# Dealing the first independent products of two pipelined stages out early instead of evenly

## The chip, the core and the metric

The kernel runs on one core of one Trainium2 chip. The metric is the device time of one execution in microseconds (us). Before the change the median of three runs is 1032.14 us (1031.85 to 1036.27). One more execution was profiled; that one took 1035.34 us, and its trace spans 1033.6 us.

## The reference, cut to what matters

One layer of a streaming encoder on 512 tokens of width 1024, all in float32:

```
x += 1/2 * SwiGLU_1(RMSNorm(x))
h  = RMSNorm(x); p = h @ W_in          # z, xbc, dt, q, k, v
     SSD: causal depthwise conv + SiLU on x/B/C, chunked scan over 16 heads, SiLU(z) gate, RMSNorm
     attention: 8 heads, own chunk + 8 previous chunks, clipped relative bias, softmax
x += concat(ssd_out, attn_out) @ W_out
x += 1/2 * SwiGLU_2(RMSNorm(x)); final RMSNorm
```

The change touches the middle only: the SSD scan and the attention, and the projections that are worked in beside them.

## The kernel before

Every float32 product is made of three matmuls on values split in a high and a low part: high by high, high by low, low by high (function `mm3`, lines 142, 143 and 144). Weights are split as they come: a cast on ScalarE writes the high part (`whi`, line 84), a subtraction on VectorE the low part (`wlo`, line 86). The weight stream `ws` splits three units ahead of their use and loads some units earlier still, by the SP queue (line 79).

The mixing stage has two halves. Each has a chain of steps whose matmuls wait for VectorE (DVE) and ScalarE (ACT), and each has a list of products that depend on no step of that chain. A generator yields after every six matmuls of such a product (or at its end, with its eviction); below, six matmuls are called a unit. An object `fill` of the class `Filler` is called at fixed places between the steps, and it takes units from the generator as they come due.

*SSD half.* There are eight steps: two head groups `g` by four chunks `c` of 128 tokens. Step by step the functions are `ssd_decay` (GpSimd, line 903, writes the tiles `fu` and `fh`), `ssd_in` (four transposes, line 914; eviction line 916; scaling of Y on ACT, line 922), `ssd_mask` (matmuls line 932, exponential line 934, DVE lines 937 to 944; from the second chunk on also line 954), `ssd_out` (lines 967 and 972; DVE 969, 977, 979) and `ssd_state` (line 987). The independent work (`fill1`) is B and C of the second group and the x columns 4 to 7 (each with a convolution: eviction line 839, ACT 845, three DVE operations of line 848, SiLU line 850), then v (`do_v`), z (gates, lines 886 to 889) and the first q and k columns. There are 87 units; 72 of them are dealt out over 35 calls, and a loop takes the other 15 at the end.

*Attention half.* There are 32 steps: eight heads by four query tiles of 128 rows, the longest first (i = 3, 2, 1, 0). `att_scores` makes the scores (lines 1189 and 1190), adds the bias and finds the row minimum (DVE, line 1193), takes the exponential (ACT, line 1197) and scales the rows (DVE, lines 1199 and 1200). Two steps later `att_transpose` transposes the result (line 1208), and ACT (line 1213) and DVE (line 1215) write its two parts; one more step later, at a head's end, `att_values` multiplies by v (line 1230; ACT 1232, DVE 1233, ACT 1234, DVE 1235). The bias of a head comes in the head's first step: a DMA issued by ACT (line 1176), then GpSimd (lines 1178 and 1179). The independent work (`fill2`) is four q and k products (16 units; evictions `do_qk`, lines 1023 to 1042), among whose last units the SSD output is scaled and split (lines 149 and 150), and the output projection of the SSD rows (32 units; evictions lines 1254 and 1255). These 48 units are dealt out over 64 calls. Before its first unit `fill2` starts the row norm of the SSD output (line 186), and it spreads it (line 205) after the fourth.

PSUM has three buffers `mm` for the products and five buffers `aux` for the chain. A tool orders each engine's instructions; TensorE (PE) stays close to the written order, while on DVE and ACT work of neighbouring steps is interleaved. Each engine works off its own instructions strictly in order.

Of the kernel before, what the change touches and what calls it, by code (L numbers as in the profile page):

```python
# [28 lines left out]
RATE1, RATE2, NPRE = 72, 48, 8  # L29
# [8 lines left out]
def hybrid_block(ctx: ExitStack, tc, xT, xt, par, wgu1, wd1, ws1, win, wdt, wv, wo, rbt, wgu2, ws2, fin, out):  # L38
# [6 lines left out]
    def sb(tag, shape, dt=F32, bufs=1):  # L45
        uid[0] += 1
        return pool.tile(shape, dt, tag=tag, name=f"{tag}_{uid[0]}", bufs=bufs)
# [41 lines left out]
    class Job:  # L89
# [3 lines left out]
        def __init__(self, split, *moves):  # L93
            self.split, self.moves, self.parts, self.holds = split, list(moves), None, self
# [52 lines left out]
    def split_act(src, wcol, hi, lo):  # L147

        S.activation(out=hi, in_=src, func=AF.Copy, scale=wcol)
        V.scalar_tensor_tensor(out=lo, in0=src, scalar=wcol, in1=f(hi), op0=ALU.mult, op1=ALU.subtract)  # L150
# [31 lines left out]
    def rstd_begin(acc, n):  # L182

        ps = aux()
        for t in range(NC):
            T.matmul(ps[:, t:t + 1], lhsT=acc[:, t * P:(t + 1) * P], rhs=ones[:, 0:1], start=True, stop=True)
        r = rstd_rows(ps, NC, n)
        return diag_parts(r, NC, sb("s51", [P, NC, P], F32R), sb("acc", [P, NC, P], F32R)), r
# [18 lines left out]
    def rstd_end(dg):  # L207

        pb = aux()
        spread(pb, dg)  # L210
        rs = sb("rstd", [P, SEQ], bufs=2)
        S.copy(out=rs, in_=pb)
        return rs
# [33 lines left out]
    def xw_slot(k):  # L247
        return lambda: xw_pair(k)
# [575 lines left out]
    def proj_gen(ah, al, done):  # L824

        ps = mmps()
        for k in range(KD):
            if k % 4 == 0:
                wh, wl = ws.get()
            mm3(ps, wh[:, k % 4], wl[:, k % 4], ah[k], al[k], k == 0, k == KD - 1)  # L830
            if k % 2 == 1 and k < KD - 1:
                yield
        done(ps)
        yield


    def conv(ci, dst, ps):
        u = sb("fa", [P, SEQ], bufs=3)
        V.tensor_tensor(out=u, in0=ps, in1=rs, op=ALU.mult)
        y = sb("fs", [P, SEQ], bufs=2)  # L840

        def cw(j):
            return pt[:, C_CW + 12 * j + ci:C_CW + 12 * j + ci + 1]

        S.activation(out=y, in_=u, func=AF.Identity, scale=cw(3), bias=pt[:, C_CB + ci:C_CB + ci + 1])
        for j in (2, 1, 0):
            d = 3 - j
            V.scalar_tensor_tensor(out=y[:, d:SEQ], in0=u[:, 0:SEQ - d], scalar=cw(j), in1=y[:, d:SEQ],
                                   op0=ALU.mult, op1=ALU.add)
        S.activation(out=dst, in_=y, func=AF.Silu)  # L850
# [3 lines left out]
    def bc(g):  # L854

        tiles = [slot(8 + 4 * g + i, None, F32) for i in range(2)]
        gens = [proj_gen(xh, xl, lambda ps, i=i: conv(8 + 2 * i + g, tiles[i], ps)) for i in range(2)]
        for i in (0, 0, 0, 1, 1, 1, 0, 1):
            next(gens[i], None)
            yield  # L860
        bf.append(tiles[0])
        cf.append(tiles[1])

    def bc_products(g):

        pa = aux()
        for c in range(NC - 1):
            T.transpose(out=pa[:, c * P:(c + 1) * P], in_=bf[g][:, c * P:(c + 1) * P], identity=ident)
        th = slot(10 + 4 * g, [P, NC - 1, P], F32)
        S.copy(out=th.rearrange("p c n -> p (c n)"), in_=pa[:, 0:384])  # L870
        btk.append(th)

        pa = aux()
        for c in range(NC):
            cs = slice(c * P, (c + 1) * P)
            T.matmul(pa[:, cs], lhsT=bf[g][:, cs], rhs=cf[g][:, cs], start=True, stop=True)
        t = slot(11 + 4 * g, [P, NC, P], F32)
        V.tensor_tensor(out=t, in0=pa.rearrange("p (c l) -> p c l", c=NC),
                        in1=tri.unsqueeze(1).broadcast_to([P, NC, P]), op=ALU.mult)
        cbm.append(t)  # L880
# [168 lines left out]
    def fill_by(names):  # L1049
        for t in names:  # L1050
            if t == 'v':
                yield from do_v()
            elif t[0] == 'z':
                yield from proj_gen(xh, xl, lambda ps: gate(int(t[1]), ps))
            else:
                yield from qk_gen(int(t[1]))

    def fill1():
        yield from bc(1)
        for i in range(4, 8):  # L1060
            yield from proj_gen(xh, xl, lambda ps: conv(i, Y[i], ps))
        yield from fill_by(FILL1)

    class Filler:
        def __init__(self, gen, total, slots):
            self.gen, self.rate, self.due = gen, total / slots, 0.0

        def __call__(self):
            self.due += self.rate
# [71 lines left out]
    T.matmul(pa[:, 0:64], lhsT=onesr, rhs=dal.rearrange("p c h -> p (c h)"), start=False, stop=True)  # L1141
    S.activation(out=cd.rearrange("p c h -> p (c h)"), in_=pa[:, 0:64], func=AF.Exp)
    steps = [dict(g=g, c=c) for g in range(2) for c in range(NC)]
    fill = Filler(fill1(), RATE1, 4 * 8 + 3)
    bc_products(0)
    ssd_decay(steps[0])
    fill()
# [89 lines left out]
    def fill2():  # L1237
        dg, _ = rstd_begin(acc3, D)
        gh, gl = [], []
        total = 8 * len(FILL2)  # L1240
        for n, _ in enumerate(fill_by(FILL2)):
            if n == total - 1 - KD // 2 - NPRE:
                rs3 = rstd_end(dg)

            for i in range(max(0, 2 * (n - total + KD // 2)), 2 * (n - total + KD // 2 + 1)):
                hi, lo = xw_slot(i)()
                split_act(Y[i], pt[:, C_SSD + i:C_SSD + i + 1], hi, lo)
                gh.append(hi)
                gl.append(lo)
            yield  # L1250

        def done(o, ps):
            t = sb("fa", [P, SEQ], bufs=3)
            V.tensor_tensor(out=t, in0=ps, in1=rs3, op=ALU.mult)
            V.tensor_tensor(out=x[:, o], in0=x[:, o], in1=t, op=ALU.add)

        for o in range(KD):
            yield from proj_gen(gh, gl, lambda ps: done(o, ps))

    steps = [dict(hd=hd, i=i) for hd in range(AH) for i in (3, 2, 1, 0)]  # L1260
    fill = Filler(fill2(), RATE2, 2 * len(steps))
    LAG, VLAG = 2, 1
    for n in range(len(steps) + LAG + VLAG):
        if n < len(steps):
# [166 lines left out]
```

## Time and profile before

| | us |
|---|---|
| median of three runs | 1032.14 |
| profiled execution | 1035.34 |
| its span | 1033.6 |
| TensorE (PE) busy | 1007.9 |
| VectorE (DVE) busy | 810.2 |
| ScalarE (ACT) busy | 587.8 |
| SSD half, with the loop at its end | about 391 to 555 |
| attention half | about 555 to 656 |

The profiled execution is 3.2 us longer than the median run. Times inside it are counted from the start of its span. A row of the timeline shows a start, a duration, the engine, the line, and in brackets how long the engine was idle before it and what ended that.

### The profile page before, as it was taken

The numbers are of one execution on the slowest core, as the hardware profiler recorded it, in microseconds if no ns is written. First come the engines' busy times: TensorE is split into PE (matmuls) and PEld (weight loads), VectorE is DVE, ScalarE is ACT, GpSimd is POOL, SyncE is SP. The second block draws the span as 40 slices with busy tenths as digits, with TensorE's granted clock in tenths as the row PEclk, the third lists the DMA queues.
The fourth block names the chain that finished last, engine by engine and source line by source line (L and its number), as shares of the span: only waits on it lengthen the run. The fifth ranks groups of instructions, "written<-read, shape, count | busy, mean of one in ns | idle before, by whom it ended". The sixth has DMA issues, their size and how long they took to land. (4 is left out here: it accounts for less than half of the span.)

```text
span 1033.6 us, 16129 instructions
## 1 busy us (share of the span) xinstructions
PE 1007.9 (98%) x6154; PEld 888.6 (86%) x6154; DVE 810.2 (78%) x1353; ACT 587.8 (57%) x926; POOL 163.7 (16%) x186
## 2 busy tenths in 40 slices
PE   8999999999999999999999999999999999999895
PEld 7889989998898777778878778879999899988884
DVE  7868876887676698978867999797688668876587
ACT  7555535654474456646656876666655356544445
POOL 1111121111110013323201111101211111111110
PEclk9999999999999999999999999999999999999988
DMA  8969989998652321222232223755898889988842
GB/s 309 290 160 210 218 185 228 224 203 211 147 122 91 102 82 62 71 73 69 71 98 71 82 83 102 230 131 128 191 211 209 196 209 231 209 213 202 167 107 99
DMA packets 48221, 162.66 MB, mean 157 GB/s; under 512 B 5264, under 2 KB 6032, under 8 KB 48144
## 3 DMA queue, kind: packets, MB, share of 16 engines
q0 software_dynamic: 16848, 60.04, 33.2%
q1 hardware_dynamic: 28992, 96.74, 27.1%
q10 hardware_dynamic: 2304, 4.86, 1.5%
q8 instruction: 48, 0.79, 0.3%
q14 instruction: 29, 0.24, 0.1%
HBM read 159.52 MB, written 2.10 MB: 156 GB/s over the span
## 5 line engine op out<-in xcount | busy, mean ns | idle before, releaser
L555 PE MATMUL mm<-s,xw 128*128 128x256 f32 x1824 | 231.6, 284 | 6.4 <-ACT fu L563 4.6
L555 PEld LDWEIGHTS mm<-s,xw 128*128 128x128 f32 x1824 | 224.9, 192 | 7.6 <-ACT fu L563 5.0
L272 ACT CAST xw<-raw 128x1024 fp32r<-128x1024 f32 (+1 forms) x127 | 131.5, 1036 | 138.3 <-PE mm L555 56.0
L274 DVE TENSOR_TENSOR xw<-raw,xw 128x1024 fp32r<-128x1024 f32 (+1 forms) x127 | 152.7, 1204 | 69.4 <-ACT xw L272 69.4
L555 PE MATMUL aux<-s,xw 128*128 128x256 f32 x1368 | 174.5, 283 | 0.6 <-DVE xw L274 0.6
L555 PEld LDWEIGHTS aux<-s,xw 128*128 128x128 f32 x1368 | 169.0, 192 | 1.9 <-DVE xw L274 0.8
L142 PE MATMUL mm<-xw,whi 128*128 128x512 f32 x364 | 149.1, 410 | 0.0
L143 PE MATMUL mm<-xw,whi 128*128 128x512 f32 x364 | 144.3, 397 | 0.0
L274 DVE TENSOR_TENSOR xw<-s,xw 128x1024 fp32r<-128x1024 f32 (+1 forms) x87 | 104.6, 1202 | 50.5 <-ACT xw L272 50.4
L144 PE MATMUL mm<-xw,wlo 128*128 128x512 f32 x364 | 144.0, 396 | 0.0
L272 ACT CAST xw<-s 128x1024 fp32r<-128x1024 f32 (+1 forms) x87 | 90.0, 1035 | 92.1 <-DMA s<-wgu 27.7
L333 POOL DMA_DIRECT2D s<-wgu x57 | 52.1, 934 | 314.6 <-DMA s<-wgu 133.6
L84 ACT CAST whi<-raw 128x512 fp32r<-128x512 f32 (+1 forms) x104 | 62.1, 601 | 65.3 <-PE mm L143 47.2
L86 DVE TENSOR_TENSOR wlo<-raw,whi 128x512 fp32r<-128x512 f32 (+1 forms) x104 | 74.3, 716 | 13.8 <-ACT whi L84 13.2
L142 PEld LDWEIGHTS mm<-xw,whi 128*128 128x128 f32 x364 | 68.5, 188 | 16.2 <-issue 2.2
L144 PEld LDWEIGHTS mm<-xw,wlo 128*128 128x128 f32 x364 | 68.4, 188 | 16.1
L143 PEld LDWEIGHTS mm<-xw,whi 128*128 128x128 f32 x364 | 68.5, 188 | 15.8 <-issue 1.2
L333 POOL DMA_DIRECT2D s<-ws x31 | 27.1, 873 | 163.3 <-DVE xw L274 65.8
L144 PE MATMUL aux<-xw,s 128*128 128x512 f32 x106 | 41.8, 394 | 0.0
L143 PE MATMUL aux<-xw,s 128*128 128x512 f32 x106 | 41.7, 394 | 0.0
L142 PE MATMUL aux<-xw,s 128*128 128x512 f32 x106 | 41.7, 394 | 0.0
L903 POOL TENSOR_TENSOR fu<-dt,tri 128x512 fp32r<-128x512 f32 x16 | 18.9, 1190 | 95.6 <-PE aux L954 45.5
(294 smaller groups left out, 1743.9 us busy)
## 6 DMA issues: line engine op xcount, KB each, us to landing
raw<-wgu SPq DMA_DIRECT2D x68, 512.0 KB, 5.8
s<-wgu POOLq DMA_DIRECT2D x57, 512.0 KB, 6.5
raw<-win SPq DMA_DIRECT2D x28, 512.0 KB, 3.5
s<-ws POOLq DMA_DIRECT2D x27, 512.0 KB, 5.7
raw<-ws SPq DMA_DIRECT2D x27, 512.0 KB, 4.7
s<-wgu SPq DMA_DIRECT2D x19, 512.0 KB, 5.0
raw<-wgu POOLq DMA_DIRECT2D x19, 512.0 KB, 6.2
raw<-wo SPq DMA_DIRECT2D x12, 512.0 KB, 3.7
```

The source lines that it names most:

```text
L84: S.copy(out=hi, in_=src)
L86: V.tensor_tensor(out=lo, in0=src, in1=f(hi), op=ALU.subtract)
L142: T.matmul(ps, lhsT=sh, rhs=mh, start=start, stop=False, skip_group_check=skip)
L143: T.matmul(ps, lhsT=sh, rhs=ml, start=False, stop=False, skip_group_check=skip)
L144: T.matmul(ps, lhsT=sl, rhs=mh, start=False, stop=stop, skip_group_check=skip)
L272: S.copy(out=hi, in_=src)
L274: V.tensor_tensor(out=lo, in0=src, in1=f(hi), op=ALU.subtract)
L333: return lambda: G.dma_start(out=get(), in_=src, accum_op=ALU.add)
L555: T.matmul(ps[:, j * HS:(j + 1) * HS], lhsT=sw[:, j, k], rhs=m, start=(p in ("P1", "P2", "P5") and j == 0 and k == 0 and n == 0), stop=(k ...
L903: G.tensor_tensor(out=r, in0=f(src[:, c, h0:h0 + 4]).unsqueeze(2).broadcast_to([P, 4, P]), in1=tri.unsqueeze(1).broadcast_to([P, 4, P]), o ...
```

## The change

The constructor of `Filler` gets a fourth number, `ahead`. The debt of units starts at `ahead` instead of zero, and the rate of a call is lowered so that the debt reaches the same total after the same number of calls. In the SSD half 3 units are ahead: the first call takes 5 units instead of 2, and the rate falls from 72/35 = 2.06 to 69/35 = 1.97 units a call. In the attention half 5 units are ahead: the first call takes 6 units instead of 1, and the rate falls from 48/64 = 0.75 to 43/64 = 0.67.

```
 class Filler:
-    def __init__(self, gen, total, slots):
-        self.gen, self.rate, self.due = gen, total / slots, 0.0
+    def __init__(self, gen, total, slots, ahead):
+
+        self.gen, self.rate, self.due = gen, (total - ahead) / slots, float(ahead)

     def __call__(self):
         self.due += self.rate
...
-    fill = Filler(fill1(), RATE1, 4 * 8 + 3)
+    fill = Filler(fill1(), RATE1, 4 * 8 + 3, 3)
...
-    fill = Filler(fill2(), RATE2, 2 * len(steps))
+    fill = Filler(fill2(), RATE2, 2 * len(steps), 5)
```

Lines behind the constructor are numbered one higher in the changed kernel.

On PE, at the start of the SSD half, this is where the first step's transposes (line 914) and its mask matmuls (line 932) stood between products before:

```order
 L144 MATMUL mm_4066<-xw_498_3404,wlo_3986 128x512
-L914 MATMUL aux_4077<-ident_66,s_543_3625 128x128
-L914 MATMUL aux_4077<-ident_66,s_544_3626 128x128
-L914 MATMUL aux_4077<-ident_66,s_545_3627 128x128
-L914 MATMUL aux_4077<-ident_66,s_546_3628 128x128
-L932 MATMUL aux_4088<-fu_4027,s_472_3234 128x512
-L932 MATMUL aux_4088<-fh_4029,s_472_3234 128x512
-L932 MATMUL aux_4094<-fu_4031,s_472_3234 128x512
-L932 MATMUL aux_4094<-fh_4033,s_472_3234 128x512
 L142 MATMUL mm_4066<-xw_499_3405,whi_3984 128x512
```

They are gone from there; four units of products stand ahead of that place. The same eight matmuls stand now behind seven units (with other numbers of their PSUM buffers):

```order
 L144 MATMUL mm_4037<-xw_504_3410,wlo_3970 128x512
+L914 MATMUL aux_4109<-ident_66,s_543_3625 128x128
+L914 MATMUL aux_4109<-ident_66,s_544_3626 128x128
+L914 MATMUL aux_4109<-ident_66,s_545_3627 128x128
+L914 MATMUL aux_4109<-ident_66,s_546_3628 128x128
+L932 MATMUL aux_4120<-fu_4027,s_472_3234 128x512
+L932 MATMUL aux_4120<-fh_4029,s_472_3234 128x512
+L932 MATMUL aux_4126<-fu_4031,s_472_3234 128x512
+L932 MATMUL aux_4126<-fh_4033,s_472_3234 128x512
 L142 MATMUL mm_4066<-xw_503_3409,whi_4038 128x512
```

They have moved 18 matmuls down. On PE, at the start of the attention half, the scores of the second step (128x384) and of the third (128x256) stood before with one unit of the first q product (`mm_5546`) between them:

```order
L144 MATMUL mm_5546<-xw_498_3404,wlo_5418 128x512
L1189 MATMUL aux_5557<-s_878_5189,s_863_5120 128x384
L1190 MATMUL aux_5557<-s_880_5191,s_863_5120 128x384
L142 MATMUL mm_5546<-xw_499_3405,whi_5416 128x512
L143 MATMUL mm_5546<-xw_499_3405,whi_5416 128x512
L144 MATMUL mm_5546<-xw_499_3405,wlo_5418 128x512
L142 MATMUL mm_5546<-xw_500_3406,whi_5416 128x512
L143 MATMUL mm_5546<-xw_500_3406,whi_5416 128x512
L144 MATMUL mm_5546<-xw_500_3406,wlo_5418 128x512
L1189 MATMUL aux_5575<-s_878_5189,s_863_5120 128x256
L1190 MATMUL aux_5575<-s_880_5191,s_863_5120 128x256
```

Now both stand back to back behind six units (half of the second product, `mm_5594`, is among them), and the first step's transposes follow at once:

```order
L144 MATMUL mm_5594<-xw_500_3406,wlo_5461 128x512
L1190 MATMUL aux_5611<-s_878_5189,s_863_5120 128x384
L1191 MATMUL aux_5611<-s_880_5191,s_863_5120 128x384
L1190 MATMUL aux_5623<-s_878_5189,s_863_5120 128x256
L1191 MATMUL aux_5623<-s_880_5191,s_863_5120 128x256
L1209 MATMUL aux_5635<-ident_66,s_947_5503 128x128 x4
L142 MATMUL mm_5594<-xw_501_3407,whi_5547 128x512
```

So scores that were spread over the first two units now come after six. On ACT, around the DMA that fetches the bias of the third head (`rbt`; line 1176, now 1177), the order was this; line 1030 belongs to a k or q eviction, lines 1213 and 1234 to attention:

```order
L1042 COPY s_1024_5721<-fs_5723 64x512
L1234 CAST s_1033_5745<-fu_5755 64x512
L1213 CAST s_983_5592<-aux_5760 128x4x128
L1197 ACTIVATE fs_5784,sm_5785<-s_1041_5781,mn_5782 128x128
L1213 CAST s_983_5592<-aux_5790 128x3x128
L84 CAST whi_5802<-raw_5704 128x512
L1176 DMA fu_5814<-rbt 128x512
```

Now it is this, where line 149 casts the scaled SSD output for the output projection:

```order
L149 ACTIVATE xw_1049_5821<-s_543_3625,par_61 128x512
L1235 CAST s_1042_5788<-fu_5798 64x512
L149 ACTIVATE xw_1050_5824<-s_544_3626,par_61 128x512
L1214 CAST s_994_5640<-aux_5839 128x3x128
L149 ACTIVATE xw_1058_5851<-s_545_3627,par_61 128x512
L149 ACTIVATE xw_1059_5854<-s_546_3628,par_61 128x512
L1177 DMA fu_5857<-rbt 128x512
L1198 ACTIVATE fs_5833,sm_5834<-s_1052_5830,mn_5831 128x128
```

The first four casts of the SSD output stand ahead of the DMA; before, they came after it.

## Rows read from the trace of the kernel before

**Rows 1.** The page: engines busy over the span (us, share, instructions).
```profile
PE 1007.9 (98%) x6154; PEld 888.6 (86%) x6154; DVE 810.2 (78%) x1353; ACT 587.8 (57%) x926; POOL 163.7 (16%) x186
```

**Rows 2.** Stretches: PE, PEld, DVE, ACT, POOL busy (count), granted TensorE clock, DMA share, GB/s.
```profile
391.00:545.00 154.00, 152.58 (x809) 122.76 (x808) 124.18 (x219) 95.56 (x158) 37.34 (x31) 1.00 0.23 72
560.00:610.00 50.00, 48.16 (x243) 39.14 (x242) 47.85 (x131) 41.93 (x92) 6.18 (x7) 1.00 0.26 80
610.00:660.00 50.00, 49.98 (x259) 41.51 (x257) 44.52 (x115) 29.93 (x70) 6.97 (x8) 1.00 0.37 110
980.58:987.40 6.82, 4.79 (x22) 4.79 (x23) 5.10 (x7) 3.00 (x4) 0.00 (x0) 0.50 0.16 30
```

**Rows 3.** What PE waited for from 391 to 545 (total, times, longest).
```profile
PE aux L914 <- ACT s L850: 0.6, 1, 0.6
PE mm L142 <- DVE fa L839: 0.6, 1, 0.6
PE aux L954 <- DVE s L969: 0.2, 1, 0.2
```

**Rows 4.** The same from 545 to 660.
```profile
PE aux L1208 <- DVE s L1200: 1.4, 1, 1.4
PE aux L1208 <- DVE fs L1200: 0.4, 1, 0.4
```

**Rows 5.** Timeline of PE around the first mask: one unit's first and last row.
```profile
399.11 0.33 PE L914 MATMUL aux<-ident,s 128*128 128x128 f32 x1 [0.65 <-ACT s L850]
399.98 0.40 PE L932 MATMUL aux<-fh,s 128*128 128x512 f32 x1
400.22 0.40 PE L142 MATMUL mm<-xw,whi 128*128 128x512 f32 x1
401.62 0.40 PE L142 MATMUL mm<-xw,whi 128*128 128x512 f32 x1
406.34 1.09 PE L972 MATMUL aux<-s,s 128*64 128x128 f32 x16
```

**Rows 6.** Timeline of DVE in the same stretch.
```profile
399.48 0.69 DVE L916 TENSOR_TENSOR s<-aux,dt 128x512 f32<-128x512 f32 x1 [1.82 <-PE aux L914]
402.17 0.73 DVE L937 COPY dt<-s 128x4 f32<-128x4 f32 x1 [2.00 <-ACT s L934]
405.53 0.68 DVE L944 TENSOR_TENSOR s<-s,dt 128x512 f32<-128x512 f32 x1
```

**Rows 7.** The wait for an mm buffer: PE and DVE.
```profile
438.02 0.39 PE L144 MATMUL mm<-xw,wlo 128*128 128x512 f32 x1
441.60 0.68 DVE L839 TENSOR_TENSOR fa<-mm,rstd 128x512 f32<-128x512 f32 x1
442.33 0.50 PE L142 MATMUL mm<-whi,xw 128*128 128x512 f32 x1 [0.60 <-DVE fa L839]
```

**Rows 8.** Timeline, the third head's bias: ACT's queue, ACT, DVE, PE.
```profile
577.66 0.33 ACTq L1176 DMA_DIRECT2D fu<-rbt  x1
582.59 1.34 ACT L149 ACTIVATE xw<-s,par 128x512 fp32r<-128x512 f32 x2
583.45 0.69 DVE L1193 CUSTOM_DVE_ANT_0 s<-aux,fh 128x512 f32<-128x512 f32 x1 [0.58 <-POOL fh L1179]
586.72 0.63 PE L1208 MATMUL aux<-ident,s 128*128 128x128 f32 x4 [1.39 <-DVE s L1200]
```

**Rows 9.** Groups of DVE instructions from 545 to 660 (busy us, mean ns).
```profile
L86 DVE TENSOR_TENSOR wlo<-raw,whi 128x512 fp32r<-128x512 f32 x29 | 19.7, 681 | 0.5 <-ACT whi L84 0.5
L150 DVE SCALAR_TENSOR_TENSOR xw<-s,par,xw 128x512 fp32r<-128x512 f32 x8 | 5.8, 743 | 0.0
L1031 DVE TENSOR_TENSOR s<-fa,s 64x512 fp32r<-64x512 f32 x6 | 4.2, 702 | 0.2
```

**Rows 10.** A late weight in the second FFN: ACT and PE.
```profile
981.03 1.04 ACT L272 CAST xw<-s 128x1024 fp32r<-128x1024 f32 x1 [6.35 <-DMA s<-wgu]
982.61 0.80 PE L555 MATMUL mm<-s,xw 128*128 128x256 f32 x2 [4.64 <-ACT fu L563]
```

## The prediction

> **What bounds the kernel now.** I read the page's first part, then the busy times by stretch, then PE's waits in the two stretches that the change touches, then the timeline around each wait. PE is busy for 98% of the span [rows 1]. Between 391 and 545 us it idles for 154.00 - 152.58 = 1.42 us, between 560 and 610 for 1.84 us, and between 610 and 660 for 0.02 us [rows 2]. These 3.3 us are all that a better order of the same work can win back by the profile, 0.3% of the run. A matmul row lasts 0.40 us, while six products take 1.40 us from start to start [rows 5], 0.23 us each, so ends overlap and a wait hides up to 0.17 us of itself; with some five waits the bound is about 4.1 us. The waits are few and named. In the SSD half a transpose waits 0.65 us for the SiLU of the last convolution, a product waits 0.60 us for a PSUM buffer that DVE has not read, and a mask matmul 0.17 us for DVE [rows 3, 5, 7]. In the attention half transposes wait 1.39 and 0.42 us for the row scaling on DVE [rows 4, 8]. There DVE is the second bound: it is busy for 47.85 of 50 us up to 610 [rows 2].
>
> **The change part by part.** No instruction on PE or DVE is added or removed; units are moved. A unit is six products, 1.40 us of PE. The lead of three units in the SSD half shrinks by 3/35 of a unit with each call, that of five units in the attention half by 5/64, and both are zero at the last call. So what lies behind both halves starts from the same amount of work done, and I look for the waits that go and those that come. Two table loads fewer on ACT count for nothing: ACT is busy for 95.56 of 154 us there [rows 2].
>
> *First transposes, SSD.* They come three units later, 3 x 1.40 = 4.2 us; the wait for the SiLU was 0.65 us. It goes: -0.65 us (between -0.8, with what the overlap hides, and 0).
>
> *First mask.* From the last mask matmul to the first product that needs the mask PE had 406.34 - 399.98 = 6.36 us [rows 5], and DVE finished just before: line 944 ran from 405.53 for 0.68 us [rows 6]. The number of units between the two stays four. But the convolution of B is now evicted ahead of the mask on DVE: line 839 and three of line 848, some 0.7 us each, 2.7 us by the nearest rows of that size (0.68 us, [rows 7]). DVE stood idle for 1.82 and 2.00 us there, waiting for the transposes and for the exponential [rows 6], and these 3.8 us cover the 2.7. I take +0.2 us (0 to +1.0, if the table load on ACT falls in the wrong place).
>
> *The PSUM buffer.* The last product of the seventh x column ends on PE at 438.02 us, DVE evicts it at 441.60, and PE goes on at 442.33 [rows 7]. Until it asked for the buffer PE had work for 442.33 - 0.60 - 438.25 = 3.5 us: one unit of v and a step's products of lines 967 and 972. In the new order it has one unit, 1.4 us, and four transposes, some 1.8 us in all (an estimate by a fourth of the 16 products of line 972, 1.09 us, [rows 5]), so it asks 1.7 us sooner, and DVE may be only half as late as it was. The 3.8 us that DVE idled at the start are now filled with evictions that it did later; that takes its lag from 3.6 to about zero to one. I take -0.5 us. Bounds: -0.95 (0.60 + 0.17 and the overlap) and, if DVE stays 3.6 us late, the 1.7 us by which PE asks sooner, +1.7 us.
>
> *Front of the attention half.* The first call takes six units, 8.4 us of PE, between the scores of the first step and of the second. The weights of these units are split three units ahead, and the loop before them takes 15 units at PE's full pace with the same stream, without a wait (from 545 to 560 no wait is among [rows 4]). The spread of the row norm stands behind the fourth unit, 5.6 us after the norm was begun, and its chain on DVE is some fourteen short operations and two of 512 columns. I take 0 us (0 to +0.7, one operation of 0.68 us, [rows 7], too late).
>
> *The bias of the third head.* PE's longest wait is here. ACT issues the DMA at 577.66, DVE's bias operation starts at 583.45 after an idle 0.58 us that GpSimd's last bias operation ends, and the transposes start at 586.72 after 1.39 us of idling [rows 8]. That is 9.1 us from the DMA's issue to the transposes. In the new ACT order four casts of line 149 stand ahead of the DMA, 0.67 us each [rows 8], 2.7 us, while the two casts of line 1030, the weight cast and the four copies of a k eviction that stood near it are done earlier. On PE the third head's first transposes have 18 units before them in the new order and 14.3 in the old one. On DVE the scaled casts (line 150, 0.74 us, [rows 9]) and an eviction stand between the bias operation and the scaling, where before it was one. So I expect the wait to stay and grow by about 0.9 us, to 2.3 us. Bounds: -1.55 if the earlier SSD casts leave ACT free in time, +3.0 if DVE, which works strictly in order, stands still behind the bias operation (0.58 us before) for the whole 2.7 us and some work of the next step queues up behind it.
>
> *The small waits behind it.* A q or k product costs DVE two splits, the eviction (like a split) and two parts: (3 x 0.68 + 2 x 0.70)/4 = 0.86 us a unit, and the SSD split adds 8 x 0.74/16 = 0.37 [rows 9]: 1.23 us against PE's 1.40. Each unit of lead gives DVE 0.17 us of room; 4 units of lead at that place make 0.7 us, more than the 0.42 us wait [rows 4]. It goes: -0.4 us (-0.6 to 0). Later the lead is handed back, with fewer units between the scores and their transposes; from 610 on PE idles for 0.02 us of 50 [rows 2], with DVE at 44.52 us. 0 us.
>
> *Sum.* -0.65 + 0.2 - 0.5 + 0 + 0.9 - 0.4 = -0.45 us. The profiled execution with the change would take 1035.34 - 0.45 = 1034.9 us; it is 3.2 us above the median run, so I put the difference on the median: 1032.14 - 0.45 = 1031.7 us. The ends of the bounds add up to -3.9 (about all waits) and +6.4 us, which would all have to come together.
>
> **The rivals.** *All waits go.* If ACT and DVE are ahead everywhere, 3.3 to 4.1 us are won: about 1028.4 us. For it speaks that each wait has DVE or ACT as its cause and that the lead is largest where the waits are; against it that the longest one hangs on a DMA which the order puts later.
>
> *The bias chain decides, and it is slower.* DVE has 2.15 us of slack in the 50 us up to 610 [rows 2]. If the bias comes 2.7 us late for the third head, DVE loses more than it has, and the work behind it (PSUM evictions too) comes late for the fourth head again: 2.7 + 2.7 us, without the other gains: 1032.14 + 5.4 = 1037.5 us. It decides from the point at which the bias operation stands idle on DVE for more than the 2.15 us of slack. Against it: the later heads' DMAs keep their place in ACT's order.
>
> The clock could add to that. After a PE wait of 4.64 us in the second FFN [rows 10] the granted clock fell to 0.50, the 1.2 GHz level, for 6.82 us [rows 2]; the waits of 0.65 and 1.39 us left it at 1.00, the 2.4 GHz level. The Trainium skill, TensorE: Matmul & The Clock Gate, section HAM oscillation, says that a PE which idles between bursts of matmuls is throttled again and starts the next burst cold; by that rule a wait grown to 4 us at the bias would be paid a second time. The trace agrees at 4.64 us and shows no fall at 1.39 us. From the rows: a wait of 4 us (2.6 more than now) and a like fall, 6.82 us at half pace, 3.4 us, would make 1032.14 + 6.0 = 1038.1 us. I count it with this rival.
>
> *The late weight.* The 4.64 us wait comes from a weight that ACT awaited for 6.35 us [rows 10], far behind the change. Of the three runs one, 1036.27, lies 4.1 us above the others, as the profiled execution does by 3.2; I take it for an estimate that such a lateness comes in some executions and not in others. If the change shifts the transfers so that it comes in most, the median is 1031.7 + 4 = 1035.7 us.
>
> *It does nothing.* Waits are exchanged one for one: 1032.1 us. It is the neighbour of my forecast and shares its chance.
>
> **How the numbers follow.** This kernel's measurement can tell about 0.5%, 5.2 us, from no change. My forecast with its neighbour, within 1030 to 1033.5 us, gets 0.62; all waits gone 0.13; the late weight 0.11; the bias chain with the clock 0.10; more gained than all the waits, for which I see no row, 0.04. Only the last lies beyond -5.2 us, and only the bias chain beyond +5.2: faster 0.04, slower 0.10, within 0.86. The range leaves out the bias chain and the gain without a row, and takes the others in: 1028.3 to 1036.3 us.
>
> **What would show it.** In the changed profile no wait of line 914 for line 850 stands in the SSD half; line 972 of the first step waits for nothing or for under 1 us; the first product of v that needs the third buffer waits for under 0.7 us. In the attention half the transposes of the third head's first step wait for DVE for some 2 us, behind an idle DVE that GpSimd releases; the wait of 0.42 us is gone. PE's idle time from the SSD half to the end of attention is about 2.8 us. I am wrong if transposes of several heads wait, if the granted clock falls inside the two halves, or if a whole step's PE time changes without a wait that shows.

## The result, and the profile after

The changed kernel takes 1041.97 us in the median of 12 runs (1036.83 to 1044.25), the kernel before 1034.01 us in 12 runs beside it. The ratio is 1.007, with a 95% interval of 1.0057 to 1.0083: **slower by about 7.2 us** (5.9 to 8.6). I had predicted 1031.7 us, 0.45 us less than before, with 0.10 on slower. The profiled execution of the changed kernel is the fastest of its runs, 1036.83 us. A second profile, further down, stands near the median.

The page's first part and the windows of the changed kernel, columns as in [rows 1, 2]; 440.03 to 443.44 is a stretch that the trace marks with another clock.

```profile
PE 1010.1 (98%) x6154; PEld 890.5 (86%) x6154; DVE 810.2 (78%) x1353; ACT 583.6 (56%) x924; POOL 165.6 (16%) x186
```

```profile
391.00:545.00 154.00, 148.82 (x779) 119.30 (x778) 119.89 (x214) 90.23 (x153) 37.73 (x29) 0.99 0.23 69
440.03:443.44 3.41, 3.29 (x8) 2.61 (x9) 2.68 (x5) 2.31 (x6) 0.00 (x0) 0.50 0.49 131
560.00:610.00 50.00, 48.43 (x240) 38.59 (x239) 47.19 (x129) 41.34 (x89) 4.09 (x5) 1.00 0.24 74
610.00:660.00 50.00, 49.71 (x259) 41.55 (x259) 45.73 (x124) 31.02 (x76) 7.46 (x9) 1.00 0.33 106
```

In the SSD half PE idles for 154.00 - 148.82 = 5.18 us, where it idled for 1.42 [rows 2], and the granted clock falls to 0.50 for 3.41 us in the middle of it. The attention half has about the idle time it had: 1.57 and 0.29 us instead of 1.84 and 0.02.

What PE waited for from 391 to 545 us, then from 545 to 660 (total, times, longest); it answers to [rows 3] and [rows 4].

```profile
PE mm L142 <- DVE fa L839: 3.1, 1, 3.1
PE mm L142 <- DVE fa L1010: 2.1, 1, 2.1
```

```profile
PE aux L1209 <- DVE fs L1201: 1.2, 3, 0.5
PE aux L1231 <- DVE s L1216: 0.3, 1, 0.3
PE aux L1231 <- DVE mn L1194: 0.2, 1, 0.2
```

The waits of line 914 and line 954 are gone. The wait for an mm buffer, 0.60 us in [rows 3], is now 3.1 us, and a second one for the same kind of buffer, 2.1 us, stands at the end of v, where line 1010 reads its sums. Five short waits in attention replace the 1.39 and 0.42 us.

**The two clocks of the SSD half.** I lay the place of the longer wait on a common start, the first matmul of line 1140 (1141 after), just ahead of the half. The buffer is the one that held x column 7, counted from 0 (the prediction's seventh x column). First PE of the kernel before, then PE and DVE of the changed one.

```profile
390.97 0.19 PE L1140 MATMUL aux<-dt,onesr 128*128 128x64 f32 x1
...
439.65 1.05 PE L967 MATMUL aux<-s,s 128*128 128x128 f32 x8
440.63 1.09 PE L972 MATMUL aux<-s,s 128*64 128x128 f32 x16
```

```profile
388.92 0.19 PE L1141 MATMUL aux<-dt,onesr 128*128 128x64 f32 x1
...
434.83 0.40 PE L144 MATMUL mm<-xw,wlo 128*128 128x512 f32 x1
...
440.15 0.79 PE L142 MATMUL mm<-whi,xw 128*128 128x512 f32 x1 [3.10 <-DVE fa L839]
...
444.53 1.05 PE L967 MATMUL aux<-s,s 128*128 128x128 f32 x8
445.52 1.09 PE L972 MATMUL aux<-s,s 128*64 128x128 f32 x16
446.54 0.50 PE L142 MATMUL mm<-whi,xw 128*128 128x512 f32 x1
```

```profile
439.41 0.68 DVE L839 TENSOR_TENSOR fa<-mm,rstd 128x512 f32<-128x512 f32 x1
```

DVE reads the x column 439.41 - 388.92 = 50.49 us after the start; before, 441.60 - 390.97 = 50.63 [rows 7]. PE asks for that buffer at 440.15 - 3.10 - 388.92 = 48.13 us; before, at 442.33 - 0.60 - 390.97 = 50.76. So **PE came 2.63 us sooner and DVE came when it always had**. The 2.63 us are the 0.65 us of the first transposes' wait, which the change had won, and the step's products of lines 967 and 972, which now run behind the wait (2.01 us, from 444.53 to 446.54).

Why DVE did not come sooner shows in its idle time at the start of the half. DVE of the changed kernel; it answers to [rows 6].

```profile
397.94 0.69 DVE L86 TENSOR_TENSOR wlo<-raw,whi 128x512 fp32r<-128x512 f32 x1 [2.33 <-ACT whi L84]
400.32 0.69 DVE L839 TENSOR_TENSOR fa<-mm,rstd 128x512 f32<-128x512 f32 x1 [1.69 <-PE mm L144]
```

Before, DVE idled for 1.82 us until the first transposes and for 2.00 us until the exponential [rows 6], 3.82 us. Now it idles for 2.33 us until ACT has cast a weight and for 1.69 us until a product ends, 4.02 us. A unit in the lead gives DVE its work only when the product of four units ends, so while PE ran ahead DVE stood still just as long. From the start to the read of the x column it idles for 5.76 us in all, by the gaps between its rows, and before for 5.35.

### The profile page after: what moved, and what is told of

Its sections match the earlier page's. It is cut to its first block, busy times and chain, and to the rows that moved or that the text cites. A ratio compares the mean times of both kernels' runs of the same rounds, so it can differ in the third digit from the quotient of the medians.

```text
span 1035.1 us, 16130 instructions
## 1 busy us (share of the span) xinstructions
PE 1010.1 (98%) x6154; PEld 890.5 (86%) x6154; DVE 810.2 (78%) x1353; ACT 583.6 (56%) x924; POOL 165.6 (16%) x186
## 5 line engine op out<-in xcount | busy, mean ns | idle before, releaser
L86 DVE TENSOR_TENSOR wlo<-raw,whi 128x512 fp32r<-128x512 f32 (+1 forms) x104 | 72.0, 693 | 19.4 <-ACT whi L84 19.1
```

The costliest lines, as they stand in the source:

```text
L86: V.tensor_tensor(out=lo, in0=src, in1=f(hi), op=ALU.subtract)
```

## The experiments

All times are against the kernel before, measured beside it on the same chip. "Lead 3, 0" is a lead of three units in the SSD half and none in attention. The lines shown are the PE waits of the SSD half (391 to 545 us) unless said otherwise.

**One half at a time.** Two kernels, one edit each:

```diff
-    fill = Filler(fill2(), RATE2, 2 * len(steps), 5)
+    fill = Filler(fill2(), RATE2, 2 * len(steps), 0)
```

> The lead of three units in the SSD half stays, that of the attention half is zero. Theory: the loss is made in the SSD half by one wait, that of the third product of v for a PSUM buffer (3.10 us), with the fall of the granted clock behind it, and by the wait of the first gate product at the end of v (2.08 us). Then this kernel is 5 to 7 us slower than before, and its profile has both waits and a clock of 0.50 near 440 us. Rival, the one of the prediction: the bias of the third head in the attention half. Then this kernel is within 1 us of before.

```diff
-    fill = Filler(fill1(), RATE1, 4 * 8 + 3, 3)
+    fill = Filler(fill1(), RATE1, 4 * 8 + 3, 0)
```

> The lead of five units in the attention half stays, that of the SSD half is zero. Theory (loss in the SSD half): within 1 us of before, -0.5 to +1.0, no clock of 0.50 before the second FFN. Rival (bias of the third head): 5 to 7 us slower than before.

Lead 3, 0: 1040.64 us, ratio 1.0056 (1.0036 to 1.0077), 5.8 us slower. Lead 0, 5: 1035.74 us, 1.0009 (0.9995 to 1.0024), 0.9 us slower and not to be told from none by these runs. Most of the loss is the SSD half's, and the bias of the third head, my rival of the prediction, falls. One expectation missed: in the profile of lead 0, 5 the clock fell to 0.50 ahead of the second FFN too, at 62.6 us, in the first FFN. Lead 3, 0 has the two waits of the changed kernel, and its windows show a clock that falls for twice as long at the first of them and once more behind the second, which ends at 479.32 us:

```profile
PE mm L142 <- DVE fa L839: 3.1, 1, 3.1
PE mm L142 <- DVE fa L1010: 2.1, 1, 2.1
```

```profile
442.86:449.69 6.83, 5.85 (x15) 4.75 (x16) 4.89 (x8) 3.23 (x7) 0.00 (x0) 0.50 0.22 77
480.40:483.81 3.41, 3.41 (x12) 2.73 (x11) 3.41 (x7) 2.27 (x6) 0.00 (x0) 0.50 0.00 0
```

**The buffer.** The changed kernel, with the third sum of v elsewhere:

```diff
-        vps = [mmps(), mmps(), mmps(), aux()]
+        vps = [mmps(), mmps(), aux(), aux()]
```

> The changed kernel, but the third of the four sums of v lies in one of the five aux buffers instead of the third mm buffer, so that it does not wait for DVE to read the seventh x column, and the gate product behind v finds a free mm buffer. The order of the work on PE is the same. Theory: the waits of 3.10 and 2.08 us are gone, the clock stays at 1.00 in the SSD half, and the kernel is within 1 us of before, 6 to 8 us faster than the changed kernel. Rival 1: DVE is late as a whole and PE waits for it at the next place (an aux buffer of a step): 1 to 3 us faster than the changed kernel only. Rival 2: the loss of the runs without a profile lies in the second FFN (late weights): 4 us slower than before.

1032.79 us, 0.9984 (0.997 to 0.9999): some 9 us faster than the changed kernel, and 1.7 us faster than before, by a bare margin (I had expected to be within 1 us of it). Both waits are gone, and one of 0.3 us is left:

```profile
PE aux L954 <- DVE s L977: 0.3, 1, 0.3
```

The same edit with lead 3, 0, and with no lead at all:

> The lead of three units in the SSD half alone, with the third sum of v in an aux buffer. Theory (the SSD lead costs only by way of the mm buffers, the attention lead costs 0.9 us by itself): the waits of lines 914, 142 and 954 in the SSD half, 1.42 us before, are all but gone, nothing is lost in the attention half: 1 to 2.5 us faster than before, by 0.5 to 1 us the fastest so far. Rival: the gain of the buffer in the kernel with both leads came from the attention half; then this one is level with before.

> No lead at all (the kernel before), with the third sum of v in an aux buffer. Theory: only its wait of 0.60 us is won, 0.5 to 1 us faster than before; the lead of the SSD half is worth the other 0.8 us, which this kernel does not have. Rival: the aux buffer itself is worth the whole gain and the lead nothing; then it is as fast as the kernel with the SSD lead and the aux buffer, 1 to 2.5 us faster than before.

Lead 3, 0: 1033.65 us, 0.999 (0.9977 to 1.0003); it has the shortest SSD half together with the kernel above, but the time is no better, so leaving out the attention lead won nothing that these runs can tell. No lead: 1037.73 us, 1.0028 (1.0012 to 1.0043), **2.9 us slower**, and both my theory and its rival are wrong there. The lateness of DVE only changed its victim; with two aux buffers held by v, a mask matmul waits for an aux buffer that line 969 has not read:

```profile
PE aux L932 <- DVE s L969: 1.4, 1, 1.4
PE aux L954 <- DVE s L977: 0.7, 1, 0.7
PE aux L914 <- ACT s L850: 0.6, 1, 0.6
```

These waits are 1.3 us more than before, and in the profile the half is 1.44 us longer, inside the interval of the runs (1.2 to 4.4 us); the rest of the 2.9 us I can't place. The buffer is thus no cure by itself, and the lead is worth something once the buffer is there.

**The second wait alone.** In the changed kernel the first gate product gets an aux buffer:

```diff
-    def proj_gen(ah, al, done):
+    def proj_gen(ah, al, done, buf=mmps):

-        ps = mmps()
+        ps = buf()
...
-                yield from proj_gen(xh, xl, lambda ps: gate(int(t[1]), ps))
+                yield from proj_gen(xh, xl, lambda ps: gate(int(t[1]), ps), aux if t == 'z0' else mmps)
```

> The changed kernel, with the sum of the first gate product in an aux buffer: the wait at the end of v (2.08 us) goes, the wait for the third buffer of v (3.10 us) stays. Theory (both waits cost, each with its share of the clock): 2 to 4 us faster than the changed kernel, 3 to 5 us slower than before. Rival 1: the first wait with its clock is all of it; no faster than the changed kernel by more than 1 us. Rival 2: only the second wait makes the clock fall; level with before.

1037.91 us, 1.0035 (1.0021 to 1.0049): 3.6 us slower than before, as the theory had it. The wait of 3.1 us is there alone. Without the second wait about half of the loss is left.

**GpSimd beside DVE.** At the fourth and sixth step line 903 is left out; GpSimd writes zeros in its place, so these kernels leave out two of the eight decays:

```diff
                 r = sb(tag, [P, 4, P], F32R, bufs=2)
+                if 4 * g + c in (3, 5):
+                    G.memset(f(r), 0.0)
+                else:
...
```

> The changed kernel, but at two of the eight SSD steps (the fourth and the sixth) GpSimd writes zeros in place of the product of line 903, so the decays of these two steps are left out: GpSimd then reads nothing from SBUF beside DVE at 430 to 435 and 468 to 473 us. Theory A: DVE is late for the third buffer of v because its operations with two SBUF inputs take 1.45 instead of 0.70 us while GpSimd reads (3 x 0.75 + 0.5 = 2.7 us). Then the wait of 3.10 us shrinks to under 0.8 us, the clock stays at 1.00 there, the wait of 2.08 us shrinks to under 0.8 too, and the kernel is 4 to 7 us faster than the changed one. Theory B: DVE is late because the order puts eight short operations of the step ahead of the eviction and PE asks sooner; contention is the same as before. Then the wait stays at 2.3 to 3.1 us and the kernel is within 2 us of the changed one.

> The kernel before, with the decays of the fourth and sixth SSD step left out (GpSimd writes zeros there). It is the control for the same edit on the changed kernel, which won some 7 us there. Theory: contention costs the kernel before little, because GpSimd's passes fall beside short operations of DVE: within 1 us of before, and the wait of 0.60 us for the buffer goes or shrinks. Rival: the edit saves time by itself, wherever it is put: 3 to 7 us faster than before.

On the changed kernel: 1034.6 us, 0.9999 (0.9985 to 1.0013), the whole loss is gone. The wait at the end of v is gone, the other is 1.3 us, between what the two theories said, and the clock stays at 1.00 there. On the kernel before: 1032.47 us, 0.9982 (0.9969 to 0.9996), 1.9 us faster, more than the theory's 1 us and less than the rival's 3. So the edit wins 1.9 us where there is 0.60 us to win from the wait, and some 7 us where the waits are long. DVE of the changed kernel beside GpSimd's reads (line 903 runs from 429.74 to 435.11 us), and the same three operations without them, with the read of the x column and PE's wait for it:

```profile
430.13 1.20 DVE L86 TENSOR_TENSOR wlo<-raw,whi 128x512 fp32r<-128x512 f32 x1
431.25 4.42 DVE L848 SCALAR_TENSOR_TENSOR fs<-fa,par,fs 128x511 f32<-128x511 f32 x3
```

```profile
433.08 2.32 DVE L848 SCALAR_TENSOR_TENSOR fs<-fa,par,fs 128x511 f32<-128x511 f32 x3 [0.29 <-ACT fs L845]
...
439.63 0.68 DVE L839 TENSOR_TENSOR fa<-mm,rstd 128x512 f32<-128x512 f32 x1
...
440.37 0.51 PE L142 MATMUL mm<-whi,xw 128*128 128x512 f32 x1 [1.34 <-DVE fa L839]
```

The three take 4.42 instead of 2.32 us. The first matmul ahead of the half stands at 390.89 us here, so DVE reads the x column 48.74 us after the start instead of 50.49, and PE asks for the buffer at 48.14, as it did (48.13): the 1.75 us by which DVE comes sooner are the 1.76 us by which the wait is shorter. But contention is not what the change brought: in the kernel before, GpSimd's pass at the same place stretches other operations, and no less.

```profile
430.06 1.33 DVE L86 TENSOR_TENSOR wlo<-raw,whi 128x512 fp32r<-128x512 f32 x1
431.32 1.12 DVE L979 TENSOR_TENSOR s<-s,s 128x128 f32<-128x128 f32 x1
432.37 1.00 DVE L937 COPY dt<-s 128x4 f32<-128x4 f32 x1
433.29 0.68 DVE L939 TENSOR_TENSOR s<-s,s 128x512 f32<-128x512 f32 x1
433.89 1.00 DVE L937 COPY dt<-s 128x4 f32<-128x4 f32 x1
```

In these traces an undisturbed line 937 takes 0.16 us, line 979 0.29 and line 86 0.69, so that is 3.2 us lost before and 2.6 us after (0.5 on line 86, 2.1 on line 848). Contention makes DVE late in both kernels; the change set how soon PE comes. My theory A, as it was written, mistook a condition for the cause.

The fourth step's pass alone:

> The changed kernel with the decays of the fourth SSD step alone left out (zeros by GpSimd); the sixth step's pass at 468 to 473 us stays. Theory: each of the two waits hangs on the GpSimd pass beside it. The wait for the third buffer of v is 1.3 us as with both passes left out, the wait at the end of v stays at 2.1 us: 2 to 4 us slower than before. Rival: the second wait is the lag that the first one left on DVE; then it goes with the first, and the kernel is level with before.

1037.65 us, 1.0032 (1.0014 to 1.0049), 3.3 us slower. The theory holds: the second wait is as long behind a first of 1.34 us as behind one of 3.10, so it is not the first one's trail.

```profile
PE mm L142 <- DVE fa L1013: 2.1, 1, 2.1
PE mm L142 <- DVE fa L839: 1.3, 1, 1.3
```

**A late DVE without any new order.** The kernel before, with four idle multiplies ahead of one eviction:

```diff
         u = sb("fa", [P, SEQ], bufs=3)
+        if ci == 7:
+            for _ in range(4):
+                V.tensor_tensor(out=u, in0=rs, in1=rs, op=ALU.mult)
         V.tensor_tensor(out=u, in0=ps, in1=rs, op=ALU.mult)
```

> The kernel before, its order unchanged, with four multiplies of 128x512 (0.60 us apart) on DVE ahead of the eviction of the seventh x column, overwritten by the eviction itself. Theory: what costs is the time between PE's request for that buffer and DVE's eviction, however it comes about. DVE gets there 2.4 us later, the wait of 0.60 us becomes 3.0, the granted clock falls behind it in the profile or in most runs, and the kernel is 3 to 5 us slower than before (2.4 us of wait and one to two windows of 3.41 us at half pace). Rival: a delay of DVE is caught up, or the wait does not touch the clock; then 0 to 2.4 us slower.

1036.64 us, 1.0022 (1.0003 to 1.0042): 2.3 us slower, less than I had expected. The wait is 2.6 us instead of 3.0, and the clock falls behind it:

```profile
PE mm L142 <- DVE fa L842: 2.6, 1, 2.6
```

```profile
447.10:450.51 3.41, 2.86 (x7) 2.31 (x8) 3.32 (x8) 1.97 (x3) 0.00 (x0) 0.50 0.50 154
```

A delay of DVE alone makes a wait at the same buffer and a fall of the clock as long. It is no copy of the change: the wait at the end of v is missing.

**A smaller lead.** Lead 1, 0:

> A lead of one unit in the SSD half, none in the attention half. Theory: the loss hangs on which work stands between the seventh x column and the third product of v, and with one unit the products of lines 967 and 972 still stand there, as before; and ten products stand between the mask of the fifth step and the end of v, as before. Waits of 0.6 to 1.2 us at the third buffer and none at the end of v, the clock at 1.00: within 1 us of before. Rival: the loss grows with the lead; a third of 5.8 us, 2 us slower.

1034.44 us, 0.9989 (0.9971 to 1.0007): level. The wait is the old one, 0.6 us, the wait of line 914 is gone, and lines 967 and 972 still run ahead of the request for the buffer. So the loss does not grow evenly with the lead; it comes with a lead that carries a step's products past the request. A lead of two was not run. Start of the half and read of the x column:

```profile
393.92 0.19 PE L1141 MATMUL aux<-dt,onesr 128*128 128x64 f32 x1
```

```profile
443.63 0.67 DVE L839 TENSOR_TENSOR fa<-mm,rstd 128x512 f32<-128x512 f32 x1
```

Here DVE does come sooner, at 49.71 us instead of 50.63, though it idles for longer until then, 6.88 us instead of 5.35: the same 73 operations take 2.7 us less, as the 13 weight splits of line 86 take 9.1 us in all, 0.70 each, instead of 11.9. So DVE's arrival hangs on two things, its idle time and which of its operations meet GpSimd's passes, and an order changes both.

**The changed kernel once more**, with no edit:

> The changed kernel once more, for a second profile. Theory: the waits of the SSD half are the same to some ns (3.10 and 2.08 us), and what differs from run to run is how many windows of 3.41 us at clock 0.50 follow them: two or more here instead of one, and a span 1 to 6 us longer. Rival: the runs differ in the second FFN alone.

One run, 1041.81 us, near the median of the changed kernel. The waits are the same to 10 ns, but I was wrong on the clock: here it does not fall in the SSD half at all. The rival fails too. Its span is 5.0 us longer than the first profile's; of that 3.28 us lie ahead of the half, -1.49 in it, 1.23 between the first scores and the second FFN, and 1.95 behind. PE behind the wait of 3.1 us, in lead 3, 0 and in this run:

```profile
443.84 0.80 PE L142 MATMUL mm<-whi,xw 128*128 128x512 f32 x1 [3.10 <-DVE fa L839]
444.43 0.63 PE L143 MATMUL mm<-wlo,xw 128*128 128x512 f32 x1
```

```profile
443.42 0.50 PE L142 MATMUL mm<-whi,xw 128*128 128x512 f32 x1 [3.09 <-DVE fa L839]
443.76 0.39 PE L143 MATMUL mm<-wlo,xw 128*128 128x512 f32 x1
```

**The account of the SSD half.** For each profile: the half's length from the matmul of line 1140 to the last of line 972, less the 134.82 us of before; PE's waits in it, less the 1.42 us of before; half of PE's time without waits at clock 0.50 (an estimate of what the low clock costs); and the sum of these two.

```
kernel                      longer   waits   clock   sum
changed                       5.32    3.75    1.65   5.40
changed, once more            3.83    3.75    0      3.75
lead 3, 0                     8.06    3.75    4.63   8.38
gate product in aux           3.08    1.67    1.70   3.37
fourth step's pass left out   2.08    2.00    0      2.00
both passes left out         -0.22   -0.08    0     -0.08
before, DVE delayed           3.04    1.83    1.43   3.26
before, sum in aux            1.44    1.31    0      1.31
lead 1, 0                    -0.84   -0.69    0     -0.69
lead 3, 5, sum in aux        -1.34   -1.15    0     -1.15
lead 3, 0, sum in aux        -1.34   -1.15    0     -1.15
before, both passes out      -1.11   -0.76    0     -0.76
lead 0, 5                     0.01    0.04    0      0.04
```

Waits and clock together give the length of the half to within 0.35 us in every one.

**The attention half, from the same profiles.** From the first scores to the second FFN the seven profiles with the lead of five units take 142.4 to 144.2 us, the seven without it 141.1 to 142.0. So this lead does cost something, 1.5 us between the medians, where the runs of lead 0, 5 alone could not tell 0.9 us from none.

## Why the prediction was wrong

*The PSUM buffer* is the step that failed: I expected the wait for that buffer to shrink by 0.5 us, and in the changed profile it grew from 0.60 to 3.10 us. It failed by one sentence: "The 3.8 us that DVE idled at the start are now filled with evictions that it did later; that takes its lag from 3.6 to about zero to one." The lag, from the start of the last product of the x column to DVE's read, was 441.60 - 438.02 = 3.58 us before [rows 7] and is 439.41 - 434.83 = 4.58 us. (438.02 is the start of that product's row; the prediction calls it the end, which changes no sum.) The idle time was not filled, it was exchanged (4.02 for 3.82 us). The other half of the step was right: I had PE ask 1.7 us sooner, counted from the column, and it asks 437.05 - 434.83 = 2.22 us behind the start of the column's last product instead of 441.73 - 438.02 = 3.71, so 1.5 us sooner. With the 1.0 us of lag the wait rose by 2.5 us, beyond my upper bound of +1.7, since I had held the lag at 3.6 at worst. No rival lost time in the SSD half either: the chance for a slower kernel stood on the bias chain.

*The end of v* was not among my steps, so the sum had it at nothing. I looked at the places where waits stood and asked whether they grow; here there was none. The lead left three units instead of five between the mask matmuls of the fifth step and the end of v, and put the first gate product straight behind it, while GpSimd's pass (467.60 to 473.1) was stretching DVE's work. That made 2.08 us; with both of GpSimd's passes left out the wait is gone, and with a lead of one unit, which leaves five units there, it does not come.

```profile
472.15 1.52 DVE L86 TENSOR_TENSOR wlo<-raw,whi 128x512 fp32r<-128x512 f32 x1
473.59 2.06 DVE L1010 TENSOR_SCALAR fa<-mm,rcol 128x512 f32<-128x512 f32 x3
```

```profile
474.48 0.47 PE L142 MATMUL mm<-xw,whi 128*128 128x512 f32 x1 [2.08 <-DVE fa L1010]
```

*The clock.* I had a fall of the clock inside the halves as a sign that I am wrong, and priced it with the bias chain. It came at the buffer. A wait of 3.10 or 3.09 us was followed by 3.41 us at 0.50 (the 1.2 GHz level) in two profiles, by 6.83 in another, by none in a fourth; one of 2.60 us by 3.41 us; one of 2.08 us by 3.41 us in one profile of four. The three waits of 1.34 and 1.40 us in the half were followed by none. The falls in the half begin between 1.0 us ahead of the wait's end and 1.4 us behind it. The rule I cited (the Trainium skill, TensorE: Matmul & The Clock Gate, section HAM oscillation: a PE that idles between bursts is throttled again) agrees in kind, but here the same wait is punished in some executions only.

*What the runs without a profile lost.* The half's length doesn't tell it alone: the second profile took 1041.81 us with no fall of the clock in the SSD half and 3.83 us of loss there. The mean granted clock was 0.9905 in the median of the 12 runs after and 0.993 in each of three other sets of runs of before, but a mean doesn't say where the clock fell; the changed kernel without the fourth step's pass had a mean of 0.991 in its profile, and no fall in the half. An estimate from the profiles: the three with both waits have the half longer by 3.83, 5.32 and 8.06 us, 5.7 in the mean, and the lead of attention costs some 1.5 us. That makes 7.2 us, as the runs have it, but by some luck, since the three differ by 4 us. One kernel does not fit: for both leads with the sum in aux the same account gives +0.2 us, and the runs gave -1.7 (-3.1 to -0.1).

*First transposes and first mask* went as forecast: the wait of line 914 is gone, and the mask waits for nothing. But the 0.65 us won there were handed to the mm buffer, where PE came sooner by just that, with the 2.01 us of lines 967 and 972 on top.

*The bias of the third head* was wrong in size and in sign. DVE's bias operation has no idle time ahead of it, and the transposes of that step wait for nothing, where they waited 1.39 us:

```profile
591.41 0.68 DVE L1194 CUSTOM_DVE_ANT_0 s<-aux,fh 128x512 f32<-128x512 f32 x1
```

```profile
594.55 0.66 PE L1209 MATMUL aux<-ident,s 128*128 128x128 f32 x4
```

*The small waits* did not go either; there are more, and shorter. Both errors cancel in the sum of waits. With the lead of attention alone, the stretch from the first scores to the second FFN was still 0.6 us longer, though the waits recorded in it were 0.2 us less in sum. Each wait hides up to 0.17 us of itself, by the overlap of rows, and three or four more of them make 0.5 to 0.7 us: an estimate that covers most of it, and that no run tested. What the lead of attention costs is thus shown, and why is open.

*The late weight* of [rows 10] stayed, 3.07 us in the changed profile, and decides nothing.

On what slowed DVE: the rows above show operations that stretch while line 903 runs on GpSimd and not while GpSimd only writes zeros, though not every one beside the pass does: line 939 at 433.29 us, with two inputs in SBUF, took its usual 0.68 us. The Trainium skill, SBUF — State Buffer, section Who interferes with whom, says that a DVE instruction with two SBUF inputs contends with a GpSimd instruction that reads SBUF, and not with one that only writes. The trace agrees, 4.42 against 2.32 us for three operations. The prediction left contention out. It stands in both kernels, and it is a part of the lag that the new order ran into: 1.75 us of it go with the pass.

## What to carry to other kernels

Moving independent work ahead on the engine that is nearly full makes that engine reach its next finite buffer sooner; it helps only as far as the engine which frees the buffer comes sooner too. So read both clocks at each such buffer, the request and the release counted from one start, for every buffer behind the change and not only where a wait stands already. A wait on PE that grows to 2.6 to 3.1 us, as here, can be paid a second time by the clock (in four of five profiles), so price it above its length.

## What the runs showed of the hardware

The same wait of 3.09 to 3.10 us was followed by 0, 3.41 and 6.83 us at clock 0.50 in three profiles of the same instructions in this half, so the clock's answer differs from execution to execution; what tips it these runs don't show. In the first FFN it is the same: in the kernel before a wait of 1.79 us that ends at 63.3 us leaves the clock at 1.00, and in the second profile of the changed kernel one of 1.78 us at the same place, in work that the change does not touch, has the clock at 0.50.

```profile
60.00:70.00 10.00, 8.21 (x64) 7.82 (x65) 8.08 (x13) 6.10 (x8) 1.74 (x2) 1.00 0.72 176
```

```profile
62.75:66.16 3.41, 2.84 (x13) 2.85 (x14) 2.73 (x5) 1.13 (x3) 0.88 (x1) 0.50 0.49 162
```

In the rows beside GpSimd's pass the shortest operations were stretched most in proportion: a copy of 4 elements a row on DVE (line 937) took 1.00 us instead of 0.16, a product of 128x128 (line 979) 1.12 instead of 0.29, a weight split (line 86) 1.33 instead of 0.69. Line 939 kept its 0.68 us in the middle of them, and there it was GpSimd's row of line 903 (433.31 us) that took 1.56 us; beside an idle DVE (400.83 us) such a row took 1.04.
